# Two experts loaded ahead of the routing, logits without the norm, the tested block last

## The chip, the cores and the metric

One Trainium2 chip; the kernel runs on 1 of its cores. The metric is the device time of one execution in microseconds. Times are medians of runs on the chip; the views of the profile come from one execution that was recorded as it ran. Weights are in HBM. TensorE (PE) multiplies, VectorE (DVE), ScalarE (ACT) and GpSimd (POOL) do the rest, and SyncE (SP) issues the transfers (DMAs).

## The reference

One layer for 256 tokens of width 1024, in float32: a mixer of four branches, a cross-attention into 256 memory tokens, and a mixture of 32 experts, each followed by a LayerNorm. The last part is what the change touches:

```python
h = layer_norm(DEEPNORM_ALPHA * h + ca, ln2_g, ln2_b)     # ca: cross-attention, last weight ca_wo
ff = moe_ffn(h, router_w, router_b, moe_w1, moe_b1, moe_w2, moe_b2)
h = layer_norm(DEEPNORM_ALPHA * h + ff, ln3_g, ln3_b)
```

In `moe_ffn` each token picks the 4 experts of 32 with the largest logits `h @ router_w + router_b`, with gates that are a softmax over these four. An expert is `w1` (1024 x 2048, 8 MB), a clamped SwiGLU, and `w2` (1024 x 1024, 4 MB). The kernel reads all 384 MB of them.

## The kernel before

*Part 1* (up to the routing) goes through 64 units of 1 MB of weights. SP loads each into a raw buffer, ACT, DVE and POOL split it into a high and a low part (L154 to L158), and PE multiplies in three passes (L126, L128, L130). The last four units are `ca_wo`, worked off as halves; each half is added to `h` and the statistics of the second LayerNorm are taken along.

*The routing* follows. `ln2_norm` normalizes `h` (128 tokens at a time, n = 0 and 1), `ln2_in` transposes it into `h2T` with scale and bias of the norm, `logits` multiplies with the router's weights (L1183), `choose` finds the four largest (DVE), `place` numbers the tokens of each expert, and experts are ranked by their number of tokens. The ranking goes as integers into `order` (L1293). From it SP reads in a register which expert to load as rank r. Rank 0 is always expert 0.

*Part 3* runs over ranks. `CAPS` gives each rank a fixed number of slots for tokens: 5 ranks of 128, 11 of 64, 16 of 32. `GROUPS` sets the order in which ranks are worked off; ranks of a group (128, or 64+32+32, or 64+64, or 64) share one gather. Per expert: `gather_mm` (L1254) picks the tokens by a one-hot matrix into `xg`; `up` (L1367) multiplies with 8 tiles of w1; `swiglu`; `transpose_act` (L1392); `down` (L1430) multiplies with 4 tiles of w2; `scatter` (L1412) prepares a matrix of gates; `combine` (L1451) adds the result into `acc`. PE's order in one iteration is up of rank i, scatter and down of the rank before, gather of the next group, transposes of i, combine of the rank before.

*The loads.* Each expert is 12 loads of 1 MB, 8 tiles of w1 (L1013) and 4 of w2 (L1017), all issued by SP in one fixed order, the stream. They go into a ring of 19 buffers, which in part 1 held other things; a load into a buffer waits until what lay there has been read. `load_experts(n)` issues the stream up to load n. The first 12 (expert 0) need no routing result. SP works its queue strictly in order: a load that waits holds all behind it.

*The tested block* is `more_tokens` (L1458 on). If some expert has more tokens than its rank has slots, a branch is taken that works off the rest, 64 tokens at a time, with loads of its own issued by ACT. It stands behind rank number `MORE_AT` = 16 of the order, and the loads are issued so that the ring is not refilled past it until then. At the end LN3 (L1561 to L1588) normalizes `acc` and SP stores the output.

## Time and profile before

| | us |
|---|---|
| median of 3 runs | 1472.93 (1472.35 to 1474.71) |
| the profiled execution, time | 1476.52 |
| the profiled execution, span from first to last instruction | 1474.8 |
| PE busy (matmul) | 1314.4 (89%) |
| DVE busy | 543.1 (37%) |
| ACT busy | 326.2 (22%) |
| POOL busy | 225.6 (15%) |
| bytes moved | 481.04 MB, 326 GB/s over the span |

A matmul's busy time includes the time in which it streams a weight tile as its moving operand; a busy PE is not a PE at its peak, and what it waits for is read from the waits. The DMA columns of the slices and of the windows say how fast data came at each place of the span. Times within the kernel are given from the start of the span.

### The profile page before, as it was taken

Reading aid. Unit: us, or ns where it says so; the run is one execution under the profiler, and the core shown is the slowest. Engines: PE = TensorE matmul, PEld = TensorE weight load, DVE = VectorE, ACT = ScalarE, POOL = GpSimd, SP = SyncE. Lnnn points to the kernel's source line nnn. Section 1 sums busy time; section 2 is a strip of 40 time slices with the busy share of each in tenths; the row PEclk is TensorE's granted clock in tenths of the full one; section 3 lists DMA queues with packets and bytes.
Section 4 is the critical chain, followed back from the end, with each engine's and each line's share of the span. In section 5 each row is a group of like instructions: output and inputs, shape, how many; then the busy total and the mean of one; then the engine's idle time right before and its main releaser. Section 6 shows DMA issues by size and latency. Waiting matters only on the chain. (4 is left out here: it accounts for less than half of the span.)

```text
span 1474.8 us, 19331 instructions
## 1 busy us (share of the span) xinstructions
PE 1314.4 (89%) x7717; PEld 762.2 (52%) x7717; DVE 543.1 (37%) x884; ACT 326.2 (22%) x478; POOL 225.6 (15%) x132
## 2 busy tenths in 40 slices
...
GB/s 229 129 158 136 91 143 176 221 189 176 192 249 291 285 233 386 418 417 417 415 416 417 418 417 415 417 418 407 338 415 416 417 418 417 415 417 417 417 417 266
DMA packets 85457, 481.04 MB, mean 326 GB/s; under 512 B 8800, under 2 KB 9200, under 8 KB 44176
## 3 DMA queue, kind: packets, MB, share of 16 engines
...
q8 instruction: 62, 1.02, 0.3%
...
## 5 line engine op out<-in xcount | busy, mean ns | idle before, releaser
L1367 PE MATMUL ps_h<-w,xg 128*32 128x512 f32 (+2 forms) x2048 | 435.3, 633 | 47.7 <-DMA w<-in_moe_w 47.7
L1367 PEld LDWEIGHTS ps_h<-w,xg 128*32 128x32 f32 (+2 forms) x2048 | 140.5, 136 | 319.3 <-issue 212.3
L1430 PE MATMUL ps_y<-w,at 128*32 128x512 f32 (+2 forms) x1024 | 236.4, 682 | 37.6 <-DMA w<-in_moe_w 34.2
L1376 DVE TENSOR_SCALAR act<-ps_h 128x512 f32<-128x512 f32 (+1 forms) x37 | 25.4, 687 | 500.9 <-PE ps_h L1367 500.9
L156 POOL TENSOR_TENSOR w_lo<-w_f,w_hi 128x640 fp32r<-128x640 f32 (+1 forms) x64 | 162.7, 2547 | 227.9 <-ACT w_hi L154 219.3
L1430 PEld LDWEIGHTS ps_y<-w,at 128*32 128x32 f32 (+2 forms) x1024 | 69.1, 139 | 181.7 <-issue 93.6
L1574 POOL TENSOR_TENSOR r<-r,b 128x512 f32<-128x512 f32 x2 | 3.0, 1495 | 1002.6 <-ACT r L1573 1002.6
L158 DVE TENSOR_TENSOR w_lo<-w_f,w_hi 128x1408 fp32r<-128x1408 f32 x63 | 117.4, 1866 | 68.0 <-ACT w_hi L154 67.7
L154 ACT CAST w_hi<-w_f 128x2048 fp32r<-128x2048 f32 x63 | 120.0, 1906 | 101.4 <-DMA w_f<-in_w_in 33.9
L1414 ACT COPY ta<-ps_sc 128x256 f32<-128x256 f32 (+1 forms) x32 | 11.8, 369 | 455.1 <-PE ps_sc L1412 455.1
L371 DVE SCALAR_TENSOR_TENSOR convacc<-u,cols,convacc 128x256 f32<-128x256 f32 x120 | 90.3, 753 | 2.5
L1451 PE MATMUL acc<-y,ta 32*128 32x512 f32 (+2 forms) x256 | 76.9, 648 | 6.4 <-DVE y L1440 3.5
L126 PE MATMUL ps_mm<-hT_hi,w_hi 128*128 128x256 f32 x512 | 74.7, 289 | 5.2 <-ACT hT_hi L303 2.2
L130 PE MATMUL ps_mm<-hT_hi,w_lo 128*128 128x256 f32 x512 | 73.8, 288 | 2.4 <-POOL w_lo L156 1.6
L128 PE MATMUL ps_mm<-hT_lo,w_hi 128*128 128x256 f32 x512 | 74.0, 288 | 0.0
L126 PEld LDWEIGHTS ps_mm<-hT_hi,w_hi 128*128 128x128 f32 x512 | 67.0, 194 | 8.2 <-issue 3.1
L130 PEld LDWEIGHTS ps_mm<-hT_hi,w_lo 128*128 128x128 f32 x512 | 67.6, 196 | 3.0 <-POOL w_lo L156 2.0
L128 PEld LDWEIGHTS ps_mm<-hT_lo,w_hi 128*128 128x128 f32 x512 | 67.5, 196 | 0.6 <-DVE hT_lo L306 0.6
L1254 PEld LDWEIGHTS ps_g<-sg,h 128*128 128x128 f32 x448 | 55.8, 206 | 16.6 <-issue 9.0
L1254 PE MATMUL ps_g<-sg,h 128*128 128x128 f32 (+1 forms) x448 | 58.5, 293 | 2.1 <-DVE act L1383 1.8
L1377 ACT ACTIVATE sg<-act 128x512 f32<-128x512 f32 (+1 forms) x37 | 23.3, 630 | 157.6 <-DVE act L1376 156.8
L1451 PEld LDWEIGHTS acc<-y,ta 32*128 32x128 f32 (+2 forms) x256 | 27.3, 196 | 33.4 <-issue 22.1
(386 smaller groups left out, 1261.2 us busy)
## 6 DMA issues: line engine op xcount, KB each, us to landing
w<-in_moe_w SPq DMA_DIRECT2D x384, 1024.0 KB, 19.9
w_f<-in_w_in SPq DMA_DIRECT2D x36, 1024.0 KB, 4.9
w_f<-in_w_branch SPq DMA_DIRECT2D x8, 1024.0 KB, 4.9
w_f<-in_ca_wk SPq DMA_DIRECT2D x4, 1024.0 KB, 5.5
w_f<-in_w_out SPq DMA_DIRECT2D x4, 1024.0 KB, 5.0
w_f<-in_ca_wq SPq DMA_DIRECT2D x4, 1024.0 KB, 4.8
w_f<-in_ca_wv SPq DMA_DIRECT2D x4, 1024.0 KB, 4.9
w_f<-in_ca_wo SPq DMA_DIRECT2D x4, 1024.0 KB, 5.7
```

What stands on the lines that cost most here:

```text
L126: PE.matmul(out, wh(i), xh(i), start=first and i == ks[0], stop=False)
L128: PE.matmul(out, wh(i), xl(i), start=False, stop=False)
L130: PE.matmul(out, wl(i), xh(i), start=False, stop=last and i == ks[-1])
L154: A.copy(hi, self.raw)
L156: G.tensor_tensor(lo[:, :n], self.raw[:, :n], hi.bitcast(F32)[:, :n], ALU.subtract)
L158: V.tensor_tensor(lo[:, n:], self.raw[:, n:], hi.bitcast(F32)[:, n:], ALU.subtract)
L371: V.scalar_tensor_tensor(ca[:, c, :], u[:, c, j:j + T], col("caw", 4 * j + c), ca[:, c, :], ALU.mult, ALU.add)
L1254: PE.matmul(pss[k // 4][:, k % 4 * w:(k % 4 + 1) * w], h[:, n, k * P:(k + 1) * P], sg[:, n, :w], start=n == 0 and k % 4 == 0, stop=n == NT ...
L1367: PE.matmul(up_out(cap, hp_, m, i), x[:, k, :], w[:, c:c + 512], start=False, stop=k == KD - 1, skip_group_check=True)
L1376: V.tensor_scalar(g, hg, LIMIT, None, ALU.min)
L1430: PE.matmul(o, at[:, k, :], w[:, q * 512:(q + 1) * 512], start=k < (2 if cap == 32 else 1), stop=k >= KD - (2 if cap == 32 else 1), skip_g ...
L1451: PE.matmul(acc[n][q], a, b, start=False, stop=last, skip_group_check=True)
```

## The change

The change has five parts.
- Experts 0 and 31 (`AHEAD`) become ranks 0 and 1, with 64 slots each, and are loaded without a routing result. `CAPS` has 2 x 64, 4 x 128, 10 x 64 and 16 x 32 slots, and `GROUPS` begins with the group of these two.
- The ring has one buffer more (`v`, which held `h2T`), so 20. The buffer `b` holds `gb2` (scale and bias of the second norm, as rows for all partitions) until the experts, where it held the router's weights before; these have tiles of their own now.
- The logits are computed from `h` before the norm: `rwg` is the router's weights times the norm's scale, and mean and standard deviation enter behind the product (`choose`). Transposes (`h_in`) and `logits` stand between the halves of the last projection. `h` is normalized without scale and bias; the first gather reads it so, and after it POOL multiplies `h` by the scale and adds the bias in place.
- The rank transposes (`by_rank_t`, `by_rank`) and the residual come behind the first up, and the first gather is cut in two around the ranking's last matmul. The products with `b2` (`bias2`) come after the first ranks of 128 slots.
- The tested block moves from rank 16 to the last iteration, between combine of the rank before last and up of the last. Scale and bias of the third norm (`gb3`) are loaded in the stream ahead of the last w1, where they came behind the last load.

```diff
-CAPS = [128] * 5 + [64] * 11 + [32] * 16
-
-GROUPS = "ABBABABABABCBSB"
-KINDS = {"A": (128,), "B": (64, 32, 32), "C": (64, 64), "S": (64,)}
+AHEAD = [0, NE - 1]
+
+CAPS = [64] * 2 + [128] * 4 + [64] * 10 + [32] * 16
+
+GROUPS = "CBBABABABABCBB"
+KINDS = {"A": (128,), "B": (64, 32, 32), "C": (64, 64)}
 FB = 64
-MORE_AT = 16
...
+                half(pss[0][0], 0, w2[0], range(8), True, True)
+                eva_o(2, 0, pss[0][0])
+                h_in(0, 0, 4)
+                half(pss[1][0], 0, w2[1], range(8), True, True)
+                eva_o(3, 0, pss[1][0])
+                ln2_stats(0)
+                yield
+                h_in(1, 0, 4)
+                half(pss[0][1], 1, w2[0], range(8), True, True)
+                eva_o(2, 1, pss[0][1])
+                h_in(0, 4, 8)
+                half(pss[1][1], 1, w2[1], range(4), True, False)
+                logits(0, 0, 8)
+                logits(1, 0, 4)
+                h_in(1, 4, 6)
+                half(pss[1][1], 1, w2[1], range(4, 8), False, True)
+                ln2_norm(0)
+                choice[0] = choose(0)
+                next(choice[0])
+                eva_o(3, 1, pss[1][1])
+                ln2_stats(1)
+                h_in(1, 6, 8, True)
+                logits(1, 4, 6)
+                logits(1, 6, 8)
...
-    ring = ["e1", "e2", "f", "x0", "x1", "k", "m", "raw0", "raw1", "hi1", "lo1", "hi2", "lo2", "hi0", "lo0", "ah", "al", "b", "n"]
+    ring = ["e1", "e2", "f", "x0", "x1", "k", "m", "raw0", "raw1", "hi1", "lo1", "hi2", "lo2", "hi0", "lo0", "ah", "al", "v", "b",
+            "n"]
...
-        if r is not None:
-            stream += [(0, r, k) for k in range(KD)]
-        if i != 1:
-            stream += [(1, units[max(i - 1, 0)][0], k) for k in range(KD // 2)]
-    w1, w2, index = [[] for _ in range(NE)], [[] for _ in range(NE)], {0: 0}
+        first = [(0, r, k) for k in range(KD)] if r is not None else []
+        second = [(1, units[i - 1][0], k) for k in range(KD // 2)] if i else []
+
+        stream += second + [(2, None, 0)] + first if i == NE - 1 else first + second
+    w1, w2, index, gb3 = [[] for _ in range(NE)], [[] for _ in range(NE)], {}, []
...
-        if r == 0:
-            return t[name][0, rows, :]
+        if r < len(AHEAD):
+            return t[name][AHEAD[r], rows, :]
...
+            elif which == 2:
+                w = slot(where, [P, 2, D], "gb3")
+                for j in range(2):
+                    S.dma_start(w[:, j, :], t["ln3_" + "gb"[j]].rearrange("(o d) -> o d", o=1).to_broadcast([P, D]))
+                gb3.append(w)
...
-    misc = slot("b", [P, 2 * D], "misc")
-    rw = misc[:, 0:KD * NE].rearrange("p (k e) -> p k e", k=KD)
-    rb = misc[:, KD * NE:(KD + 1) * NE]
+    rwf, rwg = (p3.tile([P, KD, NE], F32, name=n) for n in ("rw", "rwg"))
+    rb = p3.tile([P, NE], F32, name="rb")
+
+    rsum = p3.tile([NE, 2], F32, name="rsum")
+    rgb = p3.tile([P, 2, NE], F32, name="rgb")
+    gb2 = slot("b", [P, 2, D], "gb2")
...
+        for j in range(2):
+            S.dma_start(gb2[:, j, :], t["ln2_" + "gb"[j]].rearrange("(o d) -> o d", o=1).to_broadcast([P, D]))
+        o = _COLS["ln2g"]
+        G.tensor_tensor(rwg, rwf, cols[:, o:o + KD, None].to_broadcast([P, KD, NE]), ALU.mult)
...
+        ps = pax.tile([NE, 2], F32, tag="ax", name="ps_rs")
+        for k in range(KD):
+            PE.matmul(ps, rwf[:, k, :], cols[:, o + k:o + k + KD + 1:KD], start=k == 0, stop=k == KD - 1)
+        V.tensor_copy(rsum, ps)
...
+        ps = pax.tile([P, 2, NE], F32, tag="ax", name="ps_rgb")
+        for j in range(2):
+            PE.matmul(ps[:, j, :], rsum[:, j:j + 1].to_broadcast([NE, P]), ident[:NE, :NE], start=True, stop=True)
+        V.tensor_scalar(rgb[:, 0, :], ps[:, 0, :], -1.0, None, ALU.mult)
+        V.tensor_tensor(rgb[:, 1, :], ps[:, 1, :], rb, ALU.add)
...
+        mean, rstd = mr2[n]
+        nmr = p3.tile([P, 1], F32, tag="l2nm", name="l2nm", bufs=2)
+        V.reciprocal(rstd, rstd)
+        V.tensor_scalar(nmr, mean, rstd, -1.0, ALU.mult, ALU.mult)
+        A.activation(h[:, n, :], h[:, n, :], AF.Identity, bias=nmr, scale=rstd)
+
+    def h_in(n, k0, k1, on_v=False):
+
+        ps = psum().rearrange("p a (b c) -> p (a b) c", c=P)
+        for k in range(k0, k1):
+            PE.transpose(ps[:, k - k0, :], h[:, n, k * P:(k + 1) * P], ident)
+        (V.tensor_copy if on_v else A.copy)(h2T[0][:, k0:k1, n * P:(n + 1) * P], ps[:, :k1 - k0, :])
+
+    def logits(n, k0, k1):
+        if k0 == 0:
+            ps_lg[n] = pax.tile([P, NE], F32, tag="ax", name="ps_lg")
+        for k in range(k0, k1):
+            PE.matmul(ps_lg[n], h2T[0][:, k, n * P:(n + 1) * P], rwg[:, k, :], start=k == 0, stop=k == KD - 1)
...
+    for n in range(NT):
+        V.tensor_tensor(sg0[:, n, :].rearrange("p (e s) -> p e s", s=FB), iota[:, None, :FB].to_broadcast([P, 2, FB]),
+                        key[:, n, AHEAD[0]:AHEAD[1] + 1:AHEAD[1] - AHEAD[0], None].to_broadcast([P, 2, FB]), ALU.is_equal)
...
+    gather_mm(acc[1], sg0, P, range(4))
     ps = pax.tile([P, 2 * NE], F32, tag="ax", name="ps_ord")
     for i in range(2):
         PE.matmul(ps[0:1, i * NE:(i + 1) * NE], ecol[0:32, i:i + 1], sel[0:32, :], start=True, stop=True)
-    next(one0)
+    gather_mm(acc[1], sg0, P, range(4, KD))
     V.tensor_copy(order[:, :2 * NE], ps[0:1, :])
 
     load_experts(len(ring) - 1)
...
+    for j in range(2):
+        for n in range(NT):
+            G.tensor_tensor(h[:, n, :], h[:, n, :], gb2[:, j, :], ALU.add if j else ALU.mult)
...
+    bias2_left = [1, 0]
+    spare, result = ring_order[len(stream):len(stream) + 2]
+    for i in range(NE):
+        r, cap = units[i]
         pr, pcap = units[i - 1] if i else (None, 0)
-
-        load_experts(min(12 * i + 36, 12 * MORE_AT + 8 + len(ring)) if i <= MORE_AT else 12 * i + 36)
-        nxt = groups[firsts[r]] if r is not None and firsts.get(r, len(groups)) < len(groups) else None
+        last = i == NE - 1
+        load_experts(12 * i + 36)
+        nxt = groups[firsts[r]] if firsts.get(r, len(groups)) < len(groups) else None
         if nxt:
             sg2 = rt.tile([P, NT, P], F32, tag="sg2", name="sg2")
             list(onehot(sg2, key, nxt))
-        if i and cap == 128:
+        if i and (cap == 128 or last):
             sc = scatter(pr, pcap, 0, "ta")
-        if i < NE:
-            hp_ = up(r, cap, xg[:, :, place_in[r]], w1[r].__getitem__)
-        if i and cap != 128:
+        if last:
+
+            combine(pcap, down(pcap, at, w2[pr].__getitem__), sc)
+            more_tokens()
+        hp_ = up(r, cap, xg[:, :, place_in[r]], w1[r].__getitem__)
+        if i and cap != 128 and not last:
             sc = scatter(pr, pcap, 0, "ta")
-        if i < NE:
-            swiglu(cap, hp_, act0)
-        if i > 1:
+        if i == 0:
+            by_rank_t()
+        if last:
+            sc = scatter(r, cap, 0, "ta")
+        swiglu(cap, hp_, act0)
+        if last:
+            A.activation(eps3, eps, AF.Sqrt)
+        if i and not last:
             y = down(pcap, at, w2[pr].__getitem__)
-        if i == NE:
-            A.activation(eps3, eps, AF.Sqrt)
         if i == 0:
+            residual(0)
+            key, gate = by_rank()
             residual(1)
         if nxt:
             pss = two_banks("ps_g")
             w = sum(c for _, c in nxt)
             gather_mm(pss, sg2, w)
             gather_out(pss, xg, w)
-        if i < NE:
-            at = transpose_act(cap, act0, at_tile(cap, "at"))
-        if i == 0:
-            y = down(cap, at, w2[r].__getitem__)
-        else:
-            combine(pcap, y, sc, i == NE)
-        if i in range(NE - 8, NE - 8 + NT):
-            bias2(i - NE + 8)
-        if i == MORE_AT:
-            more_tokens()
-    free = iter(ring_order[len(stream):])
-    g3 = slot(next(free), [P, D], "g3")
-    b3_ = slot(next(free), [P, D], "b3")
-    S.dma_start(g3, t["ln3_g"].rearrange("(o d) -> o d", o=1).to_broadcast([P, D]))
-    S.dma_start(b3_, t["ln3_b"].rearrange("(o d) -> o d", o=1).to_broadcast([P, D]))
+        at = transpose_act(cap, act0, at_tile(cap, "at"))
+        if i and not last:
+            combine(pcap, y, sc)
+        if pcap == 128 and bias2_left:
+            bias2(bias2_left.pop())
+    combine(cap, down(cap, at, w2[r].__getitem__), sc, True)
+    g3, b3_ = gb3[0][:, 0, :], gb3[0][:, 1, :]
...
```

SP's queue at the routing, before: the last load of w1[0], the four of w2[0], the load of `order`, and the first loads of w1[1]. (Names in front of an arrow are buffers written; the wait lists name queues and engines.)

```order
L1013 DMA w1_4728<-in_moe_w1 128x2048 [waits DMAHW4_49,DVE_49,Pool_49]
L1017 DMA w2_4730<-in_moe_w2 128x2x1024 [waits DMAHW1_49]
L1017 DMA w2_4732<-in_moe_w2 128x2x1024 [waits PE_49]
L1017 DMA w2_4734<-in_moe_w2 128x2x1024 [waits DMAHW2_49]
L1017 DMA w2_4736<-in_moe_w2 128x2x1024 [waits DMAHW3_49,PE_49]
L1002 TENSOR_LOAD order_4881 [waits DVE_49]
L1002 ISA x2
L1013 ISA
L1013 DMA w1_5002<-in_moe_w1 128x2048
```

The same place after: the last four of w1[1] (buffers `lo2`, `hi0`, `lo0`, `ah`), the four of w2[0] (`al`, `v`, `b`, `n`), and then the load of `order`.

```order
L1031 DMA w1_5051<-in_moe_w1 128x2048
L1031 DMA w1_5053<-in_moe_w1 128x2048 [waits DMAHW7_49,PE_49]
L1031 DMA w1_5055<-in_moe_w1 128x2048 [waits DMAHW0_49]
L1031 DMA w1_5057<-in_moe_w1 128x2048 [waits DMAHW1_49]
L1040 DMA w2_5059<-in_moe_w2 128x2x1024 [waits DMAHW2_49]
L1040 DMA w2_5061<-in_moe_w2 128x2x1024 [waits DVE_49,DMAHW3_49,PE_49,Activation_49]
L1040 DMA w2_5063<-in_moe_w2 128x2x1024 [waits DMAHW4_49,Pool_49]
L1040 DMA w2_5109<-in_moe_w2 128x2x1024 [waits DVE_49,DMAHW5_49,PE_49,Activation_49]
L1020 TENSOR_LOAD order_4636 [waits DVE_49]
L1020 ISA x2
L1031 ISA
L1031 DMA w1_5111<-in_moe_w1 128x2048 [waits DMAHW6_49,PE_49]
```

The load of `order` has moved back by eight loads, and of these w2_5061 (slot `v`) and w2_5063 (slot `b`) have waits that did not stand there: the one for the readers of `h2T`, the other for POOL.

POOL's queue at the end of part 1, before: the last splits, the branch of the tested block, and LN3.

```order
L156 TENSOR_TENSOR w_lo_4664<-w_f_4595,w_hi_4663 128x640 [waits DMAHW4_49,Activation_49]
L1459 UNCONDITIONAL_BRANCH
L1574 TENSOR_TENSOR r_24577<-r_24577,b3_24574 128x512 [waits DMAHW3_49,DMAHW4_49,DMAHW2_49,DMAHW5_49,DMAHW1_49,DMAHW6_49,DMAHW0_49,DMAHW7_49,PE_49,Activation_49]
L1574 TENSOR_TENSOR r_24577<-r_24577,b3_24574 128x512 [waits Activation_49]
L1657 UNCONDITIONAL_BRANCH
```

After:

```order
L157 TENSOR_TENSOR w_lo_4715<-w_f_4646,w_hi_4714 128x640 [waits DMAHW6_49,Activation_49]
L1397 TENSOR_TENSOR h_3006<-h_3006,gb2_3444 128x1024 [waits PE_49,Activation_49] x2
L1397 TENSOR_TENSOR h_3006<-h_3006,gb2_3444 128x1024 [waits Pool_49] x2
L1532 UNCONDITIONAL_BRANCH
L1648 TENSOR_TENSOR r_23965<-r_23965,gb3_8836 128x512 [waits DMAHW4_49,DMAHW0_49,DMAHW7_49,PE_49,Activation_49]
L1648 TENSOR_TENSOR r_23965<-r_23965,gb3_8836 128x512 [waits Activation_49]
```

Four operations on the whole of `h` are new; the first waits for PE (the last record of the gather) and ACT (the norm), and they are the ones for which w2_5063 above waits.

PE's queue around the tested block, before, at rank 16: transposes and combine of a rank, then the test.

```order
L1392 MATMUL ps_at_7322<-ident_83,act0_5090 128x128 [waits DVE_49,Activation_49]
L1392 MATMUL ps_at_7322<-ident_83,act0_5090 128x128 x3
L1451 MATMUL acc00_4936<-y_7318,ta_7292 128x512
L1451 MATMUL acc01_4937<-y_7318,ta_7292 128x512 [waits DVE_49]
L1451 MATMUL acc10_4938<-y_7318,ta_7292 128x512
L1451 MATMUL acc11_4939<-y_7318,ta_7292 128x512
L1458 TENSOR_LOAD order_4881 [waits DVE_49]
L1459 COMPARE_AND_BRANCH
L1459 UNCONDITIONAL_BRANCH [waits PE_49,PE_sequencer_49]
```

After, in the last iteration: the last tile of the down of the rank before last, its combine, and the test; behind the block comes up of the last rank.

```order
L1503 MATMUL ps_y_9045<-w2_8727,at_9026 32x512 [waits DMAHW5_49]
L1503 MATMUL ps_y_9045<-w2_8727,at_9026 32x512 x3
L1524 MATMUL acc00_5013<-y_9062,ta_9043 128x512 [waits DVE_49]
L1524 MATMUL acc01_5014<-y_9062,ta_9043 128x512
L1524 MATMUL acc10_5015<-y_9062,ta_9043 128x512
L1524 MATMUL acc11_5016<-y_9062,ta_9043 128x512
L1531 TENSOR_LOAD order_4636 [waits DVE_49]
L1532 COMPARE_AND_BRANCH
L1532 UNCONDITIONAL_BRANCH [waits PE_49,PE_sequencer_49]
```

The same instructions stand around the test; what has moved is the rank behind which they stand, and that down and combine of the rank before last now stand ahead of the last up.

## Rows read from the trace of the kernel before

**Rows 1.** The span in 40 equal slices of 36.87 us: GB/s moved.

```profile
GB/s 229 129 158 136 91 143 176 221 189 176 192 249 291 285 233 386 418 417 417 415 416 417 418 417 415 417 418 407 338 415 416 417 418 417 415 417 417 417 417 266
```

**Rows 2.** Windows: stretch, busy time by engine, PE's granted clock, DMA share, GB/s.

```profile
core 0: us, PE busy (x) PEld busy (x) DVE busy (x) ACT busy (x) POOL busy (x), PEclk, DMA share, GB/s
...
485.00:490.00 5.00, 4.05 (x26) 3.89 (x26) 3.19 (x24) 1.81 (x3) 0.00 (x0) 0.50 0.02 3
490.00:495.00 5.00, 5.00 (x35) 4.88 (x35) 0.71 (x5) 1.50 (x4) 0.00 (x0) 0.75 0.72 257
...
530.00:535.00 5.00, 4.03 (x37) 3.79 (x35) 0.27 (x1) 1.50 (x4) 0.00 (x0) 1.00 0.01 3
535.00:540.00 5.00, 3.25 (x4) 1.47 (x5) 2.30 (x6) 0.00 (x0) 0.00 (x0) 0.68 0.00 0
540.00:545.00 5.00, 5.00 (x13) 2.10 (x12) 0.00 (x0) 0.00 (x0) 0.00 (x0) 0.98 0.33 103
...
480.00:600.00 120.00, 110.75 (x514) 54.88 (x513) 27.12 (x86) 10.99 (x24) 0.00 (x0) 0.92 0.79 312
600.00:700.00 100.00, 81.34 (x467) 28.46 (x464) 20.38 (x45) 9.48 (x21) 0.00 (x0) 0.87 1.02 417
...
1030.00:1045.00 15.00, 13.16 (x98) 3.86 (x94) 1.41 (x6) 0.58 (x1) 0.00 (x0) 1.00 0.52 200
...
1400.00:1450.00 50.00, 35.42 (x180) 7.07 (x180) 6.35 (x11) 2.48 (x5) 0.00 (x0) 0.78 1.02 415
```

**Rows 3.** Waits of SP: line, waited for; us in total, times, longest.

```profile
SPq L1459 <- SPq L1459: 19.1, 3, 14.2
SPq L1002 <- DVE r_ex L1217: 17.0, 1, 17.0
```

**Rows 4.** SP's queue in order of time, around the routing: start, us, issues.

```profile
465.93 6.84 SPq L1017 DMA_DIRECT2D w<-in_moe_w  x4
490.30 52.22 SPq L1013 DMA_DIRECT2D w<-in_moe_w  x16
```

**Rows 5.** PE in order of time, first ranks: 128, 64 and 32 slots.

```profile
498.10 27.63 PE L1367 MATMUL ps_h<-w,xg 128*128 128x512 f32 x64
...
536.75 15.70 PE L1430 MATMUL ps_y<-w,at 128*128 128x512 f32 x32 [2.73 <-DVE at L1394]
...
552.84 13.90 PE L1367 MATMUL ps_h<-w,xg 128*64 128x512 f32 x64
...
575.73 7.04 PE L1367 MATMUL ps_h<-w,xg 128*32 128x512 f32 x64
...
583.08 7.09 PE L1430 MATMUL ps_y<-w,at 128*64 128x512 f32 x32
```

**Rows 6.** PE in order of time, last projection, logits and first gather.

```profile
474.99 1.12 PE L130 MATMUL ps_mm<-w_hi,oT_lo 128*128 128x256 f32 x8
475.95 1.87 PE L1183 MATMUL ps_lg<-misc,h2T 128*128 128x32 f32 x16
...
480.53 3.53 PE L1183 MATMUL ps_lg<-misc,h2T 128*128 128x32 f32 x16
...
488.94 5.50 PE L1254 MATMUL acc<-sg,h 128*128 128x128 f32 x32
```

**Rows 7.** POOL in order of time: scale and bias on `h`.

```profile
377.57 2.39 POOL L1097 TENSOR_TENSOR h<-h,bc_ln_g 128x1024 f32<-128x1024 f32 x1
380.04 2.41 POOL L1098 TENSOR_TENSOR h<-h,bc_ln_b 128x1024 f32<-128x1024 f32 x1
382.39 3.41 POOL L1097 TENSOR_TENSOR h<-h,bc_ln_g 128x1024 f32<-128x1024 f32 x1
385.88 3.26 POOL L1098 TENSOR_TENSOR h<-h,bc_ln_b 128x1024 f32<-128x1024 f32 x1
```

**Rows 8.** PE in order of time, around the tested block.

```profile
1005.54 3.60 PE L1451 MATMUL acc<-y,ta 128*128 128x512 f32 x8
1015.61 0.62 PE L1361 MATMUL ps_h<-b,sel 96*32 96x512 bf16 x4 [6.47 <-issue]
```

**Rows 9.** The chain that ended last, its end.

```profile
1428.67 20.09 DMA w<-in_moe_w
1448.76 0.04 issue
1448.81 1.98 PE ps_y L1430 x8
...
1452.22 3.79 PE acc L1451 x8
...
1456.57 4.55 PE ps_y L1430 x32
```

**Rows 10.** Costliest groups of the page: the ups, with PE's idle time ahead of them.

```profile
L1367 PE MATMUL ps_h<-w,xg 128*32 128x512 f32 (+2 forms) x2048 | 435.3, 633 | 47.7 <-DMA w<-in_moe_w 47.7
```

**Rows 11.** DMA issues of the page: KB each, us from issue to landing.

```profile
w_f<-in_w_in SPq DMA_DIRECT2D x36, 1024.0 KB, 4.9
```

More of the change, by code (lines that the diff above doesn't have):

```diff
@@ L1219, in gates_of @@
         V.tensor_scalar(gate[:, n, :], ex, s2, None, ALU.mult)
-    A.activation(scr, eps, AF.Exp)
-    c0 = choose(0, logits(0))
-    next(c0)
-    ln2_in(1)
-    m0, ex0 = next(c0)
+    step(2)
+    assert not chains, chains
+    h2T[0] = slot("v", [P, KD, T], "h2T")
+    A.activation(scr, eps, AF.Sqrt)
+    load_experts(12)
+    step(2)
+    ln2_norm(1)
+    m0, ex0 = next(choice[0])
+    A.activation(scr, eps, AF.Exp)
+    c1 = choose(1)
+    next(c1)
+    place(0, m0)
+    m1, ex1 = next(c1)
+    place(1, m1)
+    ex0, ex1 = exps(*ex0), exps(*ex1)
     pm4s.close()
```

130 lines of the change are left out of this document (56 added, 74 removed).

## The prediction

> **What bounds the kernel now.** I read the slices of the span first, then the windows of the second half, then SP's waits, then the chain at the end. The slices show two kernels in one: in the first 15 (to 553 us) the DMA engines move 91 to 291 GB/s; from the 17th on they move 415 to 418, but for two slices with 407 and 338 and the last one [rows 1]. The windows give the ceiling: 417 GB/s over 600 to 700 us, 415 still over 1400 to 1450 [rows 2]. So 1 MB (1.0486 million bytes) takes 2.515 us, and an expert of 12 such loads 30.2 us. Behind the last load there is only a tail: PE multiplies the last expert, combines it, and the last LayerNorm follows. From the routing on, then, the time is the bytes at 417 GB/s, plus whatever time the DMA engines stand idle, plus the tail. I price the change by idle DMA time.
>
> There are three idle places, and two windows hold them. From 480 to 600 the engines move 312 GB/s over 120 us; at 417 the same bytes take 89.8 us, so 30.2 us are lost. From 1030 to 1045 they move 200, and 15 x (1 - 200/417) = 7.8 us are lost [rows 2]. Sum 38.0 us.
> - 480 to 492 is the routing. SP issues its twelfth load, then loads the order of the experts into a register, for which it waits 17.0 us (the view names the last DVE line it saw; the wait is that for `order`) [rows 3], and its next issue is at 490.30 [rows 4]. The window 490 to 495 moves 257 GB/s, which is 3.1 us of flow, so data flows from 491.9, 1.6 us behind the issue [rows 2].
> - 525 to 580 is slot shortage. Expert 0 has 128 slots; its up takes PE to 525.7 and its down runs from 536.75 for 15.70 us [rows 5]. Loads can only go into slots that PE has left, and the windows from 530 to 545 move 3, 0 and 103 GB/s [rows 2].
> - 1030 to 1045 is the tested block. SP waits there until its outstanding loads have landed, 14.2 us at the longest [rows 3], before it issues more.
>
> **The change part by part.**
>
> *Two experts known beforehand, 64 slots each.* Loads 13 to 20 need no routing result any more. They need slots. Loads 13 to 17 take slots that the last projection's weights and inputs hold, load 18 the slot of `h2T` (read last by the logits), load 19 the slot of `gb2`, load 20 slot `n`; all stand ahead of the load of `order` on SP's queue, which works in order. The last record of that projection ends at 476.1 and the logits of the second half at 484.06 [rows 6]. In the change two matmul groups are added earlier (10 small ones; by the logits' 1.87 us for 16 that is 1.2 us), and POOL gets small constants; I take 1.5 us of delay up to here (0.5 to 3). Transposes and logits are moved between the halves of the projection, so some 2.6 us more stand ahead of its last record: 480.2. Behind it remain statistics, two transposes, one copy and four logits, about 2.2 us: logits end at 482.4. So slots for loads 13 to 18 come at 476 to 483, while load 12 is still landing at about 481.5: these six flow without a gap, until 481.5 + 6 x 2.515 = 496.6.
>
> *The wait that is added.* Load 19 needs slot `b`, and there `gb2` lies until POOL has multiplied and shifted `h` in place: four operations of 128x1024, which may not start before the gather, which reads `h` as it was, has ended. [...] With the logits at 482.4 the gather ends at 482.4 + 4.9 + 5.5 = 492.8. The same operation on POOL (`h` times and plus a row of constants) took 2.39 and 2.41 us, and 3.41 and 3.26 beside busy DVE [rows 7]. Four at 2.4: 502.4; plus 1.6 from issue to flow: 504.0. The queue behind load 19 holds everything: load 20, the load of `order`, every later load. So the DMA idles from 496.6 to 504.0, 7.4 us. At 3.3 each it is 11.0 us; with the gather 2 us later 13; if POOL were done by 495, nothing. I take 7.5, by the quiet rows, since DVE then has only short work.
> The 3.3 to 3.4 us stood beside DVE operations with both inputs in SBUF. [...]
>
> *The start of the experts.* The first two experts now cost PE 13.90 for the up of 64 slots and 7.09 for the down, where 128 took 27.63 and 15.70 [rows 5]. With scatter, transposes, the gather and combine that is 25 to 28 us against 30.2 of DMA. Up(0) starts at about 498 and leaves a slot each 1.74 us; load 21 wants the first at 509. Up(1) is done by about 530, when load 29 wants its slots; down(0) by about 540, load 37 asks at 550. I find no load that meets an occupied slot, so the loss from 525 to 580 (about 19 of the 30.2) goes, and nothing of it comes back.
>
> *The tested block comes last.* All loads are issued ahead of it, so SP's wait for them costs no issue: 7.8 us go. What stays is PE's own stop: behind a combine it stands idle for 6.47 us before the next up, released by nothing that the trace shows ("issue") [rows 8]. It now stands between combine(30) and up(31). Let T be the last landing. The last piece of w2[30] lands 13 loads earlier, at T - 32.7; down and combine take 4 us, the block 6.5: T - 22. Three tiles of w1[31] have landed by then; PE uses one in 0.88 us (64 records of a 32-slot up in 7.04 [rows 5]) and has caught up by T - 19, 9 us before the last w1 tile. The landing of loads hides it. If the cover were gone, it would cost 6.5 us.
> [...]
>
> *gb3 in the stream.* 1 MB now lies ahead of w1[31] where before it came behind the last weight, beside the tail: +2.5 us.
>
> *The tail.* Before, the last piece of w2[30] landed at 1448.76, so the last load, four later, at about 1458.8. The last down ended 2.3 us behind that, because combine(30) held PE from 1452.22 for 3.79 and the down started at 1456.57 [rows 9]. Now combine(30) is long over and the down follows the landings: 1.94 us for the last piece [rows 9]. Equal within 1 us; same LayerNorm.
>
> *At nothing.* The 1 MB of gb2 at about 335 us lies under PE-bound work with the DMA at 91 to 291 GB/s [rows 1]. Residual in 2 wide matmuls instead of 8, the rank transposes behind up(0), the gather's copy without scale, bias2 earlier: all on PE, ACT and DVE between 500 and 1400, where PE waits for w1 loads (47.7 us in all [rows 10]); if that cover were gone they would be 1 to 3 us of gain.
>
> **The sum.** Gain 38.0 - 7.5 (slot `b`) - 2.5 (gb3) - 1.5 (delay ahead of the routing) = 26.5 us. The profiled execution took 1476.52 us with a span of 1474.8. 1476.52 - 26.5 = 1450.0. The median of the runs is 1472.93, a ratio of 0.9976: 1446.5, with the uncertainties 1447.
>
> **The rivals.**
> - A: the gap at slot `b` doesn't come (POOL starts earlier than I place it, or is done by 495). For it: POOL has nothing else from 465 on. Against it: `h` may not change before the gather has read it, and the gather's last record can't be ahead of the logits. Gain 34: 1439 us.
> - B: the block at the end is exposed. PE would have to wait for all outstanding loads as SP did (14.2 us [rows 3]); then up(31) starts at T, and 7.04 of up, about 3 of activation, and 2.7 more of down stand behind the last landing: 13 us. For it: the same block did hold SP. Against it: PE's stop before was 6.5 us while 8 loads were outstanding, and its matmuls wait for their own tile only. It decides from a stop of about 15 us on. Gain 13.5: 1460 us.
> - C: the change doesn't keep the DMA running. If PE doesn't leave slots in time, some part of the 19 us stays. For it: PE had just 20 slots of cover, and its clock was 0.68 in one window of that stretch [rows 2]. Against it: the margins of 9 to 11 us above. Gain 7.5 if all of it stays: 1466 us; with the gap at `b` at 13 or more as well, no change.
> - D, slower than before: expert 0 or 31 has more than 64 tokens, and the tested block is entered. It would run three rounds of 64 with 12 loads each into one spare slot; a 1 MB load alone lands 4.9 us after its issue [rows 11], so 36 x 4.9 = 176 us: about 1620. It decides from the 65th token. For it: the two are fixed, not picked by count. Against it: 256 tokens with 4 choices make 32 on average, and the reference's own inputs give 12 and 41.
>
> **How the numbers follow.** Forecast 0.63 (1447, its own range 1441 to 1453), A 0.13, B 0.14, C 0.07, D 0.03. The range 1437 to 1460 holds the forecast, A, and B's lower part; C, D and the rest of B, under 2 in 10, stay outside. What this kernel's measurement can tell from no change is 0.2%, 3 us. Forecast, A, B and most of C lie beyond it on the faster side: 0.95. A rest of C (0.02) is no change. D is slower: 0.03.
>
> **What would show it.** Right: SP issues eight loads from about 466 to 505 with one long wait at the last two, which names POOL; a DMA window near 0 between 497 and 504; over 415 GB/s in every window from 510 to the last landing; no dip in the middle; the last landing about 26 us earlier, 1432. Wrong: a window under 400 GB/s between 510 and 600 (C); PE idle more than 15 us before up(31), or a tail over 18 us behind the last landing (B); no gap at 497 (A); loads issued by ACT (D).

## The result, and the profile after

The changed kernel takes 1452.8 us (1452.29 to 1453.01, 4 runs), the kernel before 1473.82 us beside it: a ratio of 0.9855, 95% interval 0.9838 to 0.9872. Measured a second time (e5 below) it is 0.9829, interval 0.9816 to 0.9843: 1452.06 against 1476.93 us. So the gain is 21.0 us the first time and 24.9 the second, where 26.5 was forecast. The profiled execution went from 1476.52 to 1452.58 us, 23.9 less.

First the slices of the span after, 36.27 us each, GB/s moved. They answer to [rows 1]: the plateau begins two slices earlier, and the slices with 407 and 338 are gone.

```profile
GB/s 231 119 173 117 117 117 177 183 236 200 186 254 246 306 418 417 417 416 415 417 417 417 416 415 417 418 417 417 415 417 417 418 416 415 417 418 418 416 413 212
```

Windows after, to be laid beside [rows 2] (stretch, busy time by engine, PE's clock, DMA share, GB/s):

```profile
480.00:600.00 120.00, 109.88 (x619) 44.94 (x617) 30.02 (x93) 14.93 (x27) 9.30 (x4) 0.97 0.95 384
...
495.00:500.00 5.00, 5.00 (x26) 1.68 (x24) 0.72 (x3) 0.00 (x0) 5.00 (x3) 1.00 0.47 191
500.00:505.00 5.00, 5.00 (x27) 1.55 (x23) 0.00 (x0) 0.00 (x0) 3.53 (x2) 1.00 0.16 19
505.00:510.00 5.00, 5.00 (x27) 2.07 (x24) 0.38 (x1) 0.00 (x0) 0.00 (x0) 1.00 0.94 382
...
530.00:535.00 5.00, 5.00 (x26) 1.66 (x24) 2.00 (x3) 0.61 (x1) 0.00 (x0) 1.00 1.00 401
...
1030.00:1045.00 15.00, 10.95 (x74) 2.69 (x70) 1.27 (x5) 0.59 (x1) 0.00 (x0) 0.93 1.01 419
```

From 480 to 600 us 384 GB/s move instead of 312, so 9.5 us are lost of 120 instead of 30.2. The shortage around 535 is gone (401 in a window that had 3), and so is the dip at 1030. What is left is one gap from 497 to 506. The timeline names it (start, us, engine, line, operation; DVE, ACT and PE's other rows left out):

```profile
482.75 21.72 SPq L1040 DMA_DIRECT2D w<-in_moe_w  x4
...
491.32 2.99 PE L1323 MATMUL acc<-sg,h 128*128 128x128 f32 x16
...
494.23 9.30 POOL L1397 TENSOR_TENSOR h<-h,gb 128x1024 f32<-128x1024 f32 x4 [28.12 <-PE acc L1323]
...
505.61 6.34 SPq L1031 DMA_DIRECT2D w<-in_moe_w  x8
```

The gather ends at 494.3, POOL's four operations take 9.30 us and end at 503.5, and only then does SP get on. SP's waits say the same, and the second row shows SP's stop at the tested block, which now holds nothing behind it:

```profile
SPq L1040 <- POOL h L1397: 19.4, 1, 19.4
SPq L1532 <- SPq L1532: 17.9, 4, 10.3
```

At the end PE's rows read as follows, beside [rows 8, 9]: combine of the rank before last, the stop of 6.46 us at the tested block, the last up, the last tile of w1, the last down and combine.

```profile
1405.62 3.78 PE L1524 MATMUL acc<-y,ta 32*128 32x512 f32 x8 [1.48 <-DVE y L1513]
...
1415.86 0.62 PE L1434 MATMUL ps_h<-b,sel 96*32 96x512 bf16 x4 [6.46 <-issue]
1416.24 8.93 PE L1440 MATMUL ps_h<-w,xg 128*32 128x512 f32 x56
1426.26 1.06 PE L1440 MATMUL ps_h<-w,xg 128*32 128x512 f32 x8 [1.09 <-DMA w<-in_moe_w]
...
1431.68 5.75 PE L1503 MATMUL ps_y<-w,at 128*32 128x512 f32 x32 [0.56 <-issue]
```

The up catches up with its loads and waits for the last w1 tile, as forecast. The surprise stands in the DMA at the same time. Windows of 1 us, after:

```profile
1425.00:1426.00 1.00, 0.17 (x4) 0.00 (x0) 0.00 (x0) 0.00 (x0) 0.00 (x0) 1.00 1.01 401
1426.00:1427.00 1.00, 0.74 (x8) 0.16 (x8) 0.00 (x0) 0.00 (x0) 0.00 (x0) 1.00 0.81 324
1428.00:1429.00 1.00, 0.00 (x0) 0.00 (x0) 0.86 (x3) 0.94 (x3) 0.00 (x0) 0.79 0.72 291
1430.00:1431.00 1.00, 0.55 (x4) 0.50 (x4) 0.31 (x1) 0.30 (x2) 0.00 (x0) 0.50 0.60 242
1432.00:1433.00 1.00, 1.00 (x8) 0.22 (x4) 0.00 (x0) 0.00 (x0) 0.00 (x0) 0.50 0.58 221
1433.00:1434.00 1.00, 1.00 (x8) 0.22 (x4) 0.00 (x0) 0.00 (x0) 0.00 (x0) 0.50 0.12 49
1435.00:1436.00 1.00, 1.00 (x12) 0.22 (x4) 0.00 (x0) 0.00 (x0) 0.00 (x0) 0.80 0.05 20
```

And the end before, where the last bytes are scale and bias of the third norm:

```profile
1456.00:1457.00 1.00, 1.00 (x7) 0.32 (x10) 0.00 (x0) 0.34 (x1) 0.00 (x0) 0.50 1.04 414
1457.00:1458.00 1.00, 1.00 (x8) 0.20 (x4) 0.00 (x0) 0.03 (x1) 0.00 (x0) 0.50 0.89 356
1458.00:1459.00 1.00, 1.00 (x12) 0.32 (x8) 0.00 (x0) 0.00 (x0) 0.00 (x0) 0.79 0.65 262
1459.00:1460.00 1.00, 1.00 (x12) 0.24 (x8) 0.00 (x0) 0.00 (x0) 0.00 (x0) 1.00 0.47 188
1460.00:1461.00 1.00, 1.00 (x12) 0.12 (x4) 0.00 (x0) 0.00 (x0) 0.00 (x0) 1.00 0.32 127
```

Before, the DMA falls from full to nothing in 4 us, after in 10. All loads were issued long before (the last at 1415.7, landing 20.7 us later). So some of the 16 DMA engines had nothing left to do at 1426, and others worked until 1436. The ten windows from 1426 move 1.96 MB in all, which take 4.7 us at 417 GB/s: 5.3 us are lost there, against 1.8 in the four windows from 1457 before. The trace keeps 16 completion events for each load, one per engine. The time from the first to the last of them, for loads that land at about these times (us):

```
                         520   600   800  1000  1025  1055  1200  1400
kernel before            0.8   1.8   2.4   4.5   4.9   1.8   1.9   3.3
changed kernel           1.6   1.8   3.3   5.2   5.3   5.9   7.3   8.9
e4 (before, no block)    1.2   2.0   2.6   4.6   4.6   5.3   6.8   8.3
e6 (after, block midway) 1.7   1.9   3.5   5.4   0.6   2.0   2.6   4.1
e9 (more code on POOL)   1.5   3.3  10.5  12.6  13.9  12.1  13.1  11.5
```

The engines drift apart as the stream goes on. In the kernel before, the drain at the tested block (the DMA runs empty while SP waits there) set them level again: 4.9 at 1025, 1.8 at 1055. The change took this drain away.

The trace also says what drives them apart. Beside the weights the DMA engines carry code: the page lists 62 packets of 16 KB and 34 of 8 KB of the kind "instruction" (code packets below). Take for each load how far its 16 events lie behind the first of them, and add this up. From 600 to 1400 us in the changed kernel the sum grows by 55.3 us, and 41 code packets start, 27 of them of 16 KB. Of the growth, 53.2 us come at loads whose first event falls between 7 us ahead of and 3.5 us behind the start of a code packet (an engine that lags still works on a load when the first has finished it). Only 2.0 us come at the rest, which is over half of the loads. Each of the 27 larger packets has within 7 us a load whose sum jumps by over 1 us (1.5 us in the median). The packets don't spread evenly: near 1431 us the first five events lie within 0.4 us of each other, the last is 9.6 us behind.

### The profile page after: what moved, and what is told of

The parts are those of the page before. It is cut to its first block, busy times and chain, and to the rows that moved or that the text cites. A ratio compares the mean times of both kernels' runs of the same rounds, so it can differ in the third digit from the quotient of the medians.

```text
span 1450.9 us, 19127 instructions
## 1 busy us (share of the span) xinstructions
PE 1281.2 (88%) x7677; PEld 737.0 (51%) x7677; DVE 527.9 (36%) x831; ACT 313.9 (22%) x432; POOL 235.1 (16%) x143
## 5 line engine op out<-in xcount | busy, mean ns | idle before, releaser
L1440 PE MATMUL ps_h<-w,xg 128*32 128x512 f32 (+2 forms) x2048 | 422.8, 640 | 51.4 <-DMA w<-in_moe_w 51.3
L1440 PEld LDWEIGHTS ps_h<-w,xg 128*32 128x32 f32 (+2 forms) x2048 | 130.8, 134 | 318.6 <-issue 199.8
L1503 PE MATMUL ps_y<-w,at 128*32 128x512 f32 (+2 forms) x1024 | 225.8, 666 | 52.0 <-DMA w<-in_moe_w 50.9
L1503 PEld LDWEIGHTS ps_y<-w,at 128*32 128x32 f32 (+2 forms) x1024 | 62.7, 134 | 189.7 <-DMA w<-in_moe_w 94.5
L1648 POOL TENSOR_TENSOR r<-r,gb 128x512 f32<-128x512 f32 x2 | 3.0, 1493 | 940.7 <-ACT r L1647 940.7
L1524 PE MATMUL acc<-y,ta 32*128 32x512 f32 (+2 forms) x256 | 73.6, 642 | 7.5 <-DVE y L1513 4.5
L1323 PE MATMUL ps_g<-sg,h 128*128 128x128 f32 x416 | 56.0, 299 | 0.3
L1513 DVE TENSOR_TENSOR y<-y,ps_y 64x512 f32<-64x512 f32 x16 | 11.0, 690 | 92.1 <-ACT y L1512 92.0
```

Source lines behind the costliest of these rows:

```text
L1323: PE.matmul(pss[k // 4][:, k % 4 * w:(k % 4 + 1) * w], h[:, n, k * P:(k + 1) * P], sg[:, n, :w], start=n == 0 and k % 4 == 0, stop=n == NT ...
L1440: PE.matmul(up_out(cap, hp_, m, i), x[:, k, :], w[:, c:c + 512], start=False, stop=k == KD - 1, skip_group_check=True)
L1503: PE.matmul(o, at[:, k, :], w[:, q * 512:(q + 1) * 512], start=k < (2 if cap == 32 else 1), stop=k >= KD - (2 if cap == 32 else 1), skip_g ...
L1524: PE.matmul(acc[n][q], a, b, start=False, stop=last, skip_group_check=True)
```

## The experiments

Three theories stood for the slow fall at the end, and for what it costs. Theory 1: the DMA engines drift apart over the unbroken stream. Theory 2: the tested block, now near the end, delays the last loads. Theory 3: the rows of gb3 load the engines unevenly. The other runs test the terms of the sum. Each is timed against the kernel before on the same chip, but e1 to e4 ran on one chip, e5 to e8 on another, e9 and e10 on a third. The changed kernel's own ratio is 0.9855 in the result above and 0.9829 in e5. That is 3.8 us apart, so a difference of that size between runs of two chips shows little. For such pairs I also take from the traces the time from the landing of the 101st of the 384 weight loads (at 709 to 737 us) to that of the last. It leaves out all that happens before, and comes out alike where it should: 720.15 and 720.18 us in the two traces of the changed kernel (e5 is the second), 722.45 in the kernel before and 722.28 in e7. Below it is called the stretch.

**e1, the tested block left out** (of the changed kernel).

```diff
             combine(pcap, down(pcap, at, w2[pr].__getitem__), sc)
-            more_tokens()
```

> The changed kernel without the tested block (the overflow path is left out altogether). In the changed kernel the DMA engines run full until 1426 us and then at 0.5 to 0.8 of their share until 1433, the last weight landing at about 1436. Theory 1: the 16 DMA engines have drifted apart during the long unbroken stream, and the slowest lands every load last; the block has nothing to do with it. Then this run stays within 1.5 us of the changed kernel (1452.8), and the slow fall of the DMA share at the end stays. Theory 2: the block at the end (PE's stop of 6.46 us and the code that is fetched again there) delays the last loads or the last up. Then this run is 2.5 to 6 us faster, and the DMA share falls from full to nothing within 3 us.

0.983 (0.9815 to 0.9844), where the changed kernel has 0.9829 (e5, on another chip) and 0.9855 (the result above). The stretch is 719.45 us, 0.7 less than in the changed kernel and not 2.5 to 6. The DMA still falls slowly at the end, from 414 GB/s at 1423 to 16 at 1432, and the engines stand as far apart at 1400 (8.9 us). The stop of PE at the block is hidden but for at most these 0.7 us, and the block does not make the slow fall. Theory 2 is out.

**e2, scale and bias of the third norm behind the last weight.**

```diff
-        stream += second + [(2, None, 0)] + first if i == NE - 1 else first + second
+        stream += second + first if i == NE - 1 else first + second
+    stream += [(2, None, 0)]
```

> The changed kernel with scale and bias of the third norm (1 MB) behind the last weight again, as in the kernel before. Theory 1 (engines drifted apart, whatever is loaded): 1 MB leaves the path to the last weight, 1.5 to 2.5 us faster than the changed kernel, and the fall of the DMA share at the end remains long. Theory 3: the rows of this transfer load some of the 16 engines more than others and so make the long fall; then 4 to 7 us faster, and the weights' share falls from full to nothing within 3 us. If the transfer behind the last weight delays the tail, no gain.

0.9808 (0.9794 to 0.9822): 0.0021 or 3.1 us less than the changed kernel in e5, on another chip and with intervals that just overlap. The stretch decides: 717.61 us, 2.5 less. The fall stays long (from 414 at 1425 to 25 at 1435). So gb3 costs its own 2.5 us, and theory 3 is out.

**e3, the ring's last two buffers swapped, scale and bias on DVE.**

```diff
-    ring = [..., "v", "b", "n"]
+    ring = [..., "v", "n", "b"]
...
-    load_experts(len(ring) - 1)
+    load_experts(len(ring) - 2)
...
-            G.tensor_tensor(h[:, n, :], h[:, n, :], gb2[:, j, :], ALU.add if j else ALU.mult)
+            V.tensor_tensor(h[:, n, :], h[:, n, :], gb2[:, j, :], ALU.add if j else ALU.mult)
```

> The changed kernel with the ring's last two buffers swapped (n before b), and the four operations that apply scale and bias to h on DVE instead of POOL. By the prediction's step the DMA gap at 497 to 506 us comes from the one load that waits for POOL (SP waited 19.4 us for it) and from nothing else. Then load 19 flows at once, load 20 waits until DVE is done at about 500 (494.3 + 1.4 + 4 x 1.1), and about 2 of the 9 us of gap stay: 6 to 7 us faster than the changed kernel (1446). Rival: the load of the order or the slots left by the first up hold the queue next; then under 3 us.

0.9797 (0.9783 to 0.9811): 0.0032 or 4.7 us less than the changed kernel in e5, 8.6 less than in the result above; 6 to 7 were expected. The window of e3:

```profile
480.00:600.00 120.00, 112.66 (x648) 47.09 (x649) 34.99 (x96) 14.01 (x27) 0.00 (x0) 0.97 0.99 401
```

401 GB/s move instead of 384 to 389, so 4.6 us are lost instead of 8.1 to 9.5. Without a gap 1.7 us are still lost there (411 GB/s, e8 below), so some 2.9 us of gap stay, where I expected 2: DVE is done with the four operations at 498.7, and the flow is back about 2 us later. The load that waits for the four operations does make the gap.

**e4, the kernel before without the tested block and its limit on loads.**

```diff
-        load_experts(min(12 * i + 36, 12 * MORE_AT + 8 + len(ring)) if i <= MORE_AT else 12 * i + 36)
+        load_experts(12 * i + 36)
...
-        if i == MORE_AT:
-            more_tokens()
```

> The kernel before without the tested block and without its limit on the loads (the overflow path is left out). The dip at 1030 to 1045 us (7.8 us of idle DMA) goes. By the prediction's sum the time falls by 7.8 us. Theory 1: the drain in the middle had re-aligned the DMA engines; without it they drift over 900 us as in the changed kernel, and the last loads land later: 3 to 5 us of the 7.8 come back at the end, so 3 to 5 us faster than before, with the DMA share at the end below 0.8 for 7 us or more instead of 4. Theory 2 or 3: 7 to 8.5 us faster, and the end looks as before.

0.9965 (0.9952 to 0.9979): 5.2 us of 1476.84, interval 3.1 to 7.1. The dip is gone, the end is not what it was (windows of e4):

```profile
1030.00:1045.00 15.00, 8.75 (x46) 1.33 (x50) 2.74 (x4) 0.90 (x2) 0.00 (x0) 0.73 1.03 413
1445.00:1446.00 1.00, 0.34 (x2) 0.34 (x4) 0.97 (x3) 0.00 (x0) 0.00 (x0) 0.50 0.90 360
1446.00:1447.00 1.00, 1.00 (x4) 0.48 (x4) 0.50 (x3) 0.00 (x0) 0.00 (x0) 0.50 0.69 279
...
1450.00:1451.00 1.00, 1.00 (x9) 0.34 (x12) 0.00 (x0) 0.37 (x1) 0.00 (x0) 0.50 0.52 209
...
1452.00:1453.00 1.00, 1.00 (x8) 0.20 (x4) 0.00 (x0) 0.00 (x0) 0.00 (x0) 0.50 0.10 41
1454.00:1455.00 1.00, 1.00 (x12) 0.12 (x4) 0.00 (x0) 0.00 (x0) 0.00 (x0) 1.00 0.02 8
```

The fall takes 10 us, and by the sum of its windows 5.5 us are lost in it, 3.7 more than before. 7.8 - 3.7 = 4.1 lies within the measured interval, 7.8 outside it. The stretch says the same without the scatter of the runs: 717.44 us instead of 722.45, so 5.0 of the 7.8 are gained and 2.8 come back. The kernel, its order and its routing are those of before; only the drain is missing. This is the cleanest of the runs: a drain in the middle costs less than its idle time, because it pays part of what the end would pay.

**e5, the changed kernel again.**

> The changed kernel once more, unchanged, to stand beside the other runs of this call on the same chip. It took 0.9855 of the kernel before; the runs without the block, with gb3 behind and with the swapped ring took 0.983, 0.9808 and 0.9797. If those differences are real, this one comes out at 0.984 to 0.987 again.

0.9829 (0.9816 to 0.9843). It lies below the range I gave, and the gain is 3.9 us greater than in the first result. The ratios of e1 to e3 above are set beside this one, though those ran on another chip than e5. It loses 8.1 us from 480 to 600:

```profile
480.00:600.00 120.00, 111.25 (x620) 43.54 (x618) 29.82 (x91) 14.01 (x26) 9.29 (x4) 0.94 0.96 389
```

**e6, the changed kernel with the block back in the middle** (ring of 19).

```diff
-    ring = [..., "al", "v", "b", "n"]
+    ring = [..., "al", "b", "n"]
...
-    spare, result = ring_order[len(stream):len(stream) + 2]
+    spare, result = "v", ring_order[len(stream)]
...
-            more_tokens()
...
+        load_experts(min(12 * i + 36, 12 * 16 + 8 + len(ring)) if i <= 16 else 12 * i + 36)
...
+        if i == 16:
+            more_tokens()
```

> The changed kernel with the tested block back behind rank 16 and its limit on the loads; the buffer v leaves the ring, so the ring has 19, and the gap at slot b begins one load (2.5 us) earlier. A sum of idle times alone: 7.8 us for the dip and 2.5 for the gap, 10.3 us slower than the changed kernel. Theory 1 (the drain re-aligns the DMA engines): of these about 3 us come back at the end, where the slow fall of the DMA share is 4 us long instead of 8 to 10: 6 to 8 us slower.

0.9893 (0.9878 to 0.9909): 0.0064 or 9.5 us more than e5. I expected 6 to 8 and missed; the number itself is nearer to the bare sum of 10.3. The windows (of e6) say why:

```profile
480.00:600.00 120.00, 111.24 (x608) 43.83 (x607) 29.83 (x91) 13.49 (x26) 9.29 (x4) 0.94 0.92 377
1000.00:1030.00 30.00, 30.00 (x116) 11.95 (x116) 4.58 (x8) 1.59 (x3) 0.00 (x0) 1.00 0.75 307
1437.00:1438.00 1.00, 0.00 (x0) 0.00 (x0) 0.97 (x2) 1.00 (x1) 0.00 (x0) 0.50 0.98 393
...
1441.00:1442.00 1.00, 1.00 (x8) 0.22 (x4) 0.00 (x0) 0.00 (x0) 0.00 (x0) 0.50 0.34 135
1442.00:1443.00 1.00, 1.00 (x9) 0.23 (x5) 0.00 (x0) 0.00 (x0) 0.00 (x0) 0.50 0.06 25
```

The gap at slot `b` is 3.5 us longer, not 2.5 (377 against 389 GB/s), and the dip costs 7.9: 11.4 in all. The fall at the end takes 6 us and loses 2.7, against 5.0 in e5: 2.3 come back. 11.4 - 2.3 = 9.1. The stretch, which holds the dip and the end but not the gap, is 725.73 us, 5.6 more than in e5, where 7.9 - 2.3 = 5.6. The drift does fall at the drain (5.4 to 0.6 in the table above) and grows anew.

**e7, the kernel before with 64 slots for expert 0.**

```diff
-CAPS = [128] * 5 + [64] * 11 + [32] * 16
-GROUPS = "ABBABABABABCBSB"
+CAPS = [64] + [128] * 5 + [64] * 10 + [32] * 16
+GROUPS = "SBBABABABABCBAB"
...
-    gather_mm(acc[1], sg0, P)
-    gather_out(acc[1], xg, P)
+    gather_mm(acc[1], sg0, 64)
+    gather_out(acc[1], xg, 64)
```

> The kernel before with 64 slots for expert 0 instead of 128 (and the groups put in an order that begins with it, two groups of 64+32+32 behind); the routing still comes ahead of load 13. By the prediction's step the windows of 3, 0 and 103 GB/s between 530 and 545 us come from the 128-slot expert, whose up and down leave slots late: then they go, and 14 to 19 us are gained over the kernel before (the gap of 11.9 us at the routing stays). Rival: the shortage comes from the late start behind the routing, whatever the slots; then under 6 us.

0.9895 (0.988 to 0.991): 15.5 us. The windows of e7 where before had 3, 0 and 103 GB/s:

```profile
530.00:535.00 5.00, 5.00 (x20) 1.54 (x18) 0.00 (x0) 0.00 (x0) 0.00 (x0) 0.73 0.69 216
535.00:540.00 5.00, 5.00 (x28) 1.64 (x26) 0.00 (x0) 0.59 (x1) 0.00 (x0) 1.00 1.00 401
540.00:545.00 5.00, 5.00 (x26) 1.68 (x24) 0.00 (x0) 0.00 (x0) 0.00 (x0) 1.00 1.02 413
```

So the larger part of the change's gain does not need the loading ahead of the routing. Half as many slots for the first expert, without a second expert known beforehand, give 15.5 us, where the whole change gives 24.9 on this chip. (Two groups of 64, 32 and 32 slots stand behind the first expert in the kernel before too.) What loading ahead would give with 128 slots, no run shows.

**e8, slot b out of the ring's first round, and e2's edit.**

```diff
-    ring = [..., "v", "b", "n"]
-    ring_order = ring * (12 * NE // len(ring) + 2)
+    ring = [..., "v", "n"]
+    ring_order = ring + (ring[:3] + ["b"] + ring[3:]) * (12 * NE // len(ring) + 2)
```

> The changed kernel with slot b out of the ring's first round and behind f in the later ones, and with gb3 behind the last weight. Load 19 goes to n, load 20 to e1 as soon as the order is known and the first up has read it; the load that waits for POOL is the 23rd, wanted at about 507 us, when POOL is done (503.5). So the gap of 9 us at 497 goes but for 1 to 2 us (7 to 8 us), and 1 MB leaves the path to the last weight (1.5 to 2.5): 8 to 10 us faster than the changed kernel, 1443 to 1445 by the first chip's times. If the register load of the order or the first up holds the queue: 3 to 5 us.

1441.54 us, 0.9763 (0.9749 to 0.9777): 0.0066 or 9.7 us less than e5 by the ratios, within what was expected. The gap is gone (windows of e8):

```profile
480.00:600.00 120.00, 114.20 (x661) 48.69 (x663) 30.40 (x93) 14.58 (x27) 9.30 (x4) 0.97 1.01 411
495.00:500.00 5.00, 5.00 (x26) 1.58 (x24) 0.00 (x0) 0.00 (x0) 5.00 (x4) 1.00 1.01 396
500.00:505.00 5.00, 5.00 (x26) 1.69 (x24) 0.00 (x0) 0.00 (x0) 2.00 (x1) 1.00 1.03 424
```

POOL still takes 9.30 us for the four operations, but the load that waits for them is the 23rd instead of the 19th. This version is faster than both kernels.

**e9, more code on POOL** (4800 memsets into an unused buffer).

```diff
+        for _ in range(150):
+            G.memset(idle[0:1, :], 0.0)
```

> The changed kernel with 150 tiny memsets on POOL ahead of each of the 32 ranks (4800 instructions into a buffer that nothing reads; POOL has nothing else to do there). What makes the DMA engines drift apart is still open. Theory 1a: code transfers, each of which occupies one engine alone (62 of 16 KB and 34 of 8 KB in the changed kernel). 4800 instructions more would add some 35 packets of 8 KB, 0.3 MB or 0.7 us over all engines; by 1a they lengthen the fall of the DMA share at the end (10 us in the changed kernel, of which 5 are lost) by 1 to 4 us, unless they happen to fall evenly on the engines; time 0 to 3 us longer. If the drift comes from the weights' own packets: no change in fall or time.

0.9943 (0.9923 to 0.9964): 0.0114 or 16.8 us more than e5's ratio, which is of another chip, and 13.0 more than the ratio of the result above. By the traces it is 13.1 us: from the landing of the 61st load (615.6 us, where the changed kernel has 615.2) to that of the last. I expected 0 to 3. The page's section on queues, e9 (the changed kernel has 62 and 34 packets there):

```profile
q8 instruction: 62, 1.02, 0.3%
q14 instruction: 71, 0.58, 0.1%
```

and its windows:

```profile
900.00:1000.00 100.00, 91.68 (x446) 36.03 (x446) 18.01 (x36) 6.54 (x12) 60.73 (x681) 0.90 1.00 407
1000.00:1100.00 100.00, 89.07 (x401) 32.65 (x398) 14.05 (x30) 5.61 (x11) 60.84 (x680) 0.93 0.99 399
...
1440.00:1441.00 1.00, 1.00 (x8) 0.00 (x0) 0.00 (x0) 0.00 (x0) 0.00 (x0) 0.50 0.30 119
1442.00:1443.00 1.00, 0.22 (x2) 0.00 (x0) 0.97 (x2) 0.68 (x2) 0.00 (x0) 0.50 0.08 33
1445.00:1446.00 1.00, 0.46 (x4) 0.28 (x4) 0.42 (x1) 0.00 (x0) 0.00 (x0) 0.50 0.07 29
1448.00:1449.00 1.00, 1.00 (x8) 0.23 (x4) 0.00 (x0) 0.00 (x0) 0.00 (x0) 0.50 0.06 25
```

0.3 MB more of code are 0.7 us of all engines' time, and they cost 13 to 17. From 1442 to 1449 the DMA moves 25 to 41 GB/s; 417 / 16 = 26, one engine alone. That engine fell 10 to 14 us behind the first (table above). At 1000 us fourteen of the 16 events lie within 1 us of each other and the last 12.6 behind: the others ran out of loads, as I read it, since new ones wait for slots, and those for the slowest engine. So 407 and 399 GB/s move in the middle of the stream. The added code packets did not spread over the engines. Nor did POOL's memsets slow DVE: it is busy for 18.01 us from 900 to 1000, against 18.43 in the changed kernel.

**e10, more code on PE** (128 matmuls of one element in each of 15 ranks, results unused).

```diff
+        if cap == 32 and not last:
+            ps = one_bank([1, 8], "ps_more")
+            for _ in range(128):
+                PE.matmul(ps[:, 0:1], ident[0:1, 0:1], ident[0:1, 0:1], start=True, stop=True)
```

> The changed kernel with 128 matmuls of one element more in each of 15 ranks of 32 slots (results unused), where PE waits for loads anyway. Each is a matmul and a weight load, so a rank has 16 KB more of code, 15 packets of 16 KB more on the code queue that has 62. By theory 1a the fall of the DMA share at the end becomes longer than 10 us, 12 to 16, and the time 1 to 4 us longer; if the drift comes from the weights' own packets, the fall stays and the time too (PE's extra 8 us a rank lie in its waits). If they don't fit in those waits, the DMA windows of 600 to 1400 us fall below 415 GB/s, and the run tells nothing of the drift.

0.9969 (0.9953 to 0.9985). The windows from 900 to 1200 us fall to 396, 398 and 382 GB/s, and SP's waits for the up rise to 185.1 us in 70 waits: the added matmuls did not fit in PE's waits. The page counts 92 code packets of 16 KB, 30 more and not 15 (the 15 was an estimate; the changed kernel has 62 for 15354 matmuls and weight loads, 248 to a packet, and a rank here 256 more). By its own terms the run tells nothing of the drift.

## Why the prediction was right, and where it was off

The direction and the range held, and the mechanism but for one step, the end of the stream. Up to the landing of the 101st load the changed kernel gains 20.3 us (736.5 to 716.2) where the sum had 30.2 - 7.5 - 1.5 = 21.2. From there to the last landing it gains 2.3 where the sum had 7.8 - 2.5 = 5.3, and behind the last landing 1.3 where the sum had none. Together these are the 23.9 us of the profiled execution. Step by step:

- *Idle DMA time is the price.* Right. From 480 us on, the idle time of [rows 2] fell by 20.7 us in the window to 600 and by 7.8 at 1030, 28.5 us in all, and the profiled execution by 23.9. The difference is mostly gb3 and the end.
- *Start of the experts, 19 us.* Right: every window of 5 us or more that I read between 510 and 1425 is above 400 GB/s (the sign asked for over 415, which several miss by a little, 401 at 530 being the lowest; none is under the 400 that would have spoken for C), and e7 gives 15.5 us for the slots alone, in a kernel that still waits for the routing. Rival C (slots stay short) is out.
- *The wait at slot b, 7.5 us.* Right in place, cause (SP waits 19.4 us for POOL; e8 takes it away, e3 most of it) and size: the windows from 495 to 510 lose 7.9 us. The gather ended at 494.3 instead of 492.8, POOL took 9.30 us instead of 9.6, the quiet price. (The sum's 4.9 and 5.5 us, from the last logits to the gather and for the gather, are those of [rows 6].) The whole window to 600 loses 9.5 us in the first trace and 8.1 in e5; it holds other losses too. The slower price of 3.3 us an operation, as beside the busy DVE of [rows 7], did not come: DVE is busy for 0.72 us of the five from 495 to 500, and the four took 2.33 us each. Rival A is out.
- *gb3, 2.5 us.* Right: the stretch of e2 is 2.5 us shorter.
- *The block at the end costs nothing.* Right (and it was not entered, all 384 loads being SP's, so rival D is out): PE's stop is 6.46 us there, as it was, PE then catches up and waits 1.09 us for the last w1 tile, and e1's stretch is only 0.7 us shorter. Rival B is out. What takes the 6.46 us of the stop itself no run shows: the trace puts them down to "issue". Five code packets start from 1408.5 to 1414.6, within or just ahead of the stop; whether PE waits for code there was not tried.
- *The tail is equal within 1 us.* This step failed. The sum took T, the last landing, to follow from the bytes at 417 GB/s. In the changed kernel the last landing comes 5.3 us later than the remaining bytes would take, before 1.8. It comes at 1436.3, where the prediction had 1432. The drift of the DMA engines was no term of the sum: 7.8 us for the drain were booked as pure gain, and e4 shows that 5.2 (3.1 to 7.1) is what taking it away is worth. The work behind the last landing is 1.3 us shorter in this execution (14.5 us, against 15.8 before), but that is not the change's doing: in e5, of the same kernel, it takes 16.0.
- *From the profiled execution to the median.* The forecast of 1450.0 for the profiled execution met 1452.58, 2.6 us off. The other 3.5 us come from the ratio 0.9976: the profiled execution before stood 3.6 us above its median, the one after stands at its median (1452.58 against 1452.8), so the factor should not have been carried over.

That code packets drive the drift is shown twice: for added code by e9 (13 to 17 us), and for the kernel's own by the growth of the lag, packet by packet, in the changed kernel's trace (53.2 of 55.3 us; e10 did not separate it). What stays open: how the packets are given to the engines, and why the two gains measured, 21.0 and 24.9 us, differ.
